# Two cache copies and a store of a decoder step, issued at another place of its program

## The chip, the cores and the metric

The kernel runs on one core of a Trainium2 chip. The metric is device time in microseconds of one execution. Five engines take part: TensorE (PE), VectorE (DVE), ScalarE (ACT), GpSimd (POOL) and SyncE (SP), which here issues most of the DMA transfers. Matrix products accumulate in eight PSUM banks, which the kernel shares out by tag.

## The reference

One step of a hybrid decoder layer. Every token gets a modulated RMS norm; `w_in` projects it; one branch is a matrix-memory recurrence (mLSTM), the other a sliding-window attention with sinks; both are gated, merged and projected. There are 1024 tokens of a prompt, and 8 samples of 4 tokens, each with a cache of 128 keys and values.

```python
def sink_attend(q, k, v, q_pos, k_pos, sinks):
    ...
    s = jnp.where(mask[None, :, None, None], s, -jnp.inf)
    mx = jnp.maximum(jnp.max(s, axis=-1, keepdims=True), sink)
    p = jnp.exp(s - mx)
    den = jnp.sum(p, axis=-1, keepdims=True) + jnp.exp(sink - mx)
    o = jnp.einsum('bnkgqs,bnskd->bnqkgd', p / den, v.astype(f32))

def layer(x, c, C0, n0, m0, k_past, v_past, ...):
    ...
    else:
        cw = k_past.shape[1]
        kk = jnp.concatenate([k_past.astype(k.dtype), k], axis=1)
        vv = jnp.concatenate([v_past.astype(v.dtype), v], axis=1)
        ...
        k_keep, v_keep = kk[:, -cw:], vv[:, -cw:]
```

What the change touches is the last line for the samples: the new caches `k_s` and `v_s` are the last 124 rows of the old ones, followed by the 4 new keys or values. Nothing in the step reads `k_s` or `v_s` afterwards; they are outputs.

## The kernel before

Activations stand with channels on the 128 partitions and tokens along the free axis, in pieces of 384, 384 and 288 tokens (the last piece holds the samples' 32). Products run in split precision: each float32 operand is cast to a high part by ScalarE (`wh_`, `t3h`) and a low part by VectorE (`wl_`, `t3l`), and three products `h_h*wh`, `h_l*wh`, `h_h*wl` are summed.

TensorE's program is written out by hand: each projection (a "job", such as `g_aq` for the attention's queries or `g_mq`, `g_mk`, `g_mv` for the memory's) issues its products one by one, and after each the object `side` may let a piece of other work in. That other work consists of Python generators in streams ("a" for the attention, "m" for gates and heads, "g", "x", "s"). A `yield lag, bank` hands back a lag in a modelled time and the PSUM tag that the next piece needs; `side.tick()` lets a piece go when its lag is over. All TensorE instructions are chained in the order in which they are written.

Up to the projections of keys and values, VectorE's and ScalarE's instructions are chained in the same way. Then `V.on = S.on = False`: from there to the output projection, a scheduler of the compiler orders the two engines by dependencies and its own costs. The same holds for SP's transfers, of which `issue()` says only that each comes after the last TensorE instruction written so far. A transfer or an instruction that is moved in the program can therefore move others.

Three pieces matter. `kv_turn()` turns the values to row form (`vnD`), writes the last 128 keys and values of the prompt (`k_p`, `v_p`), and takes the samples' new keys and values, `kns` and `vns`, out of PSUM. `unit(g, b0)` is the attention of two blocks of 128 queries for one group of heads: it loads `uqv` (queries and values) and `ukv` (keys) from DRAM, computes `sc`, masks it on VectorE (`p<-sc,cst,sink`, the maxima in `mx`, then `nmx`), takes exponentials on ScalarE (`p<-p,nmx`), transposes (`pt`) and multiplies with the values (`oT`). `sample_attention()` does the like for all samples at once (`scs`, `ps`, `pts`, `os`, `ost`), and copies the result to `osm`.

The tags of PSUM that matter are "g" (two banks, in turn for the projections' pieces) and "o" (two banks: `pt` of the second half, `oT`, and from the heads' stage on `sc` too). The mLSTM heads load `hq`, `hk`, `hv`, and the normalised tokens `hb`, by SP.

SP's transfers and those that ScalarE issues take eight completion semaphores in turn; a transfer waits until the one eight before it has landed.

Of the kernel before, what the change touches and what calls it, by code (L numbers as in the profile page):

```python
# [173 lines left out]
def body(tc, a):  # L174
    nc = tc.nc
    with ExitStack() as ctx:
# [11 lines left out]
        def pb(shape, name):  # L188
            return ps.tile(shape, F32, tag="b", bufs=2, name=name)

        def po(shape, name):
            return ps.tile(shape, F32, tag="o", bufs=2, name=name)

        def ht(shape, name, dt=F32):
            return sp.tile(shape, dt, tag="half", bufs=50, name=name)
# [51 lines left out]
        def stores(src=None):  # L247

            for e in list(due):
                if e[0] <= side.now or (src is not None and e[1].tensor is src):  # L250
                    due.remove(e)
                    issue(*e[1:])

        def dma(out, in_, late=False):
            stores(in_.tensor)
            issue(out, in_, late)
# [3 lines left out]
        def issue(out, in_, late=False, eng=None):  # L260
            ins = (eng or nc.sync).dma_start(out, in_)  # L261
            ins = getattr(ins, "ins", ins)
            if eng is None and paced:
                no_sync(ins, [last["PE"]])
            if late:
                no_sync(ins, free)
                free.clear()
            free.append(ins)

        side = Side(stores, {"m": (2, 35.0), "a": (5,8.0), "x": (2, 0.0), "s": (1, 0.0), "g": (1, 0.0)}, 1.5)  # L270
        def mm(out, lhsT, rhs, start, stop, share=1, more=False):
            n = int(np.prod(rhs.shape[1:]))
            side.now += max(n, 250) / 2400 if rhs.dtype == F32R else max(n * 4 // share, 128) / 2400
            side.products += 1
            in_order(nc.tensor.matmul(out, lhsT, rhs, start=start, stop=stop, skip_group_check=more))  # L275

        def tr(out, in_, idn):
            side.now += 0.11
            side.products += 1
            in_order(nc.tensor.transpose(out, in_, idn))  # L280
# [516 lines left out]
        def kv_turn():  # L797
            kl, kTs, vT, kns, vns = at.pop("kl"), at["kTs"], at.pop("vT"), ht([128, 128], "kns")[:NS], at["vns"]
            for p, n in enumerate((3, 3, 2)):
                tp = pb([128, 3, 128], f"vtp{p}")  # L800
                for j in range(n):
                    tr(tp[:, j], vT[p][:, j * 128:(j + 1) * 128], ident)
                vn = ht([128, 3, 128], f"avn{p}")
                S.copy(vn[:, :n], tp[:, :n])
                dma(vnD[:, 3 * p:3 * p + n], vn[:, :n])
                if p < 2:
                    yield 4.0, "b"
            dma(a["v_p"], vn[:, 1])
            tp = pb([128, 3, 128], "kvtp")
            tr(tp[:, 0], kl[:, 128:256], ident)  # L810
            tr(tp[:NS, 1], kTs, ident)
            tr(tp[:NS, 2], vT[2][:, 256:288], ident)
            kn = ht([128, 128], "kl")
            V.tensor_copy(kn, tp[:, 0])
            V.tensor_copy(kns, tp[:NS, 1])
            V.tensor_copy(vns, tp[:NS, 2])
            dma(a["k_p"], kn)
            dma(a["k_s"][0:124], a["cache_k"][4:128])
            dma(a["v_s"][0:124], a["cache_v"][4:128])
            dma(a["k_s"][124:128].rearrange("t b e -> b t e"), kns)  # L820
            dma(a["v_s"][124:128].rearrange("t b e -> b t e"), vns)

        heads_done, samples_done, units_done, products_done, plain_ends = [], [], [], [], []
        oD = [dp.tile([128, SEQ], F32, name=f"oD{g}") for g in range(4)]
# [90 lines left out]
        def sample_attention():  # L915
            qpad, vns, kTs = at["qpad"], at["vns"], at["kTs"]
            kc, vc = ([ht([128, 4, 128], f"{n}{u}") for u in range(2)] for n in ("kc", "vc"))
            smask = ht([128, 2, WIN + NS], "smask")
            sinkr = cp.tile([128, 1], F32, name="sinkr")
            for u in range(2):  # L920
                dma(kc[u], a["cache_k"][:, 4 * u:4 * u + 4])
                dma(vc[u], a["cache_v"][:, 4 * u:4 * u + 4])
            dma(smask, a["smask"])
            dma(sinkr, a["sink_rows"])
            yield 12.0, "b"
            for u in range(2):
                tq = pb([128, 4, 128], f"kctp{u}")
                for j in range(4):
                    tr(tq[:, j], kc[u][:, j], ident)
                S.copy(kc[u], tq)  # L930
                yield 3.0, "b" if u == 0 else "o"
            sc = po([128, 2, WIN + NS], "scs")
            for u in range(2):
                for w in range(4):
                    b = u * 4 + w
                    qb = qpad[:, b].rearrange("p k g t -> p (k g t)")
                    r = slice(32 * w, 32 * w + 32)
                    mm(sc[r, u, 0:WIN], qb, kc[u][:, w], start=True, stop=True)
                    mm(sc[r, u, WIN:], qb, kTs, start=True, stop=True)
            p = ht([128, 2, WIN + NS], "ps")  # L940
            mx = cp.tile([128, 2], F32, name="mxs")
            for u in range(2):
                V.tensor_tensor_reduce(p[:, u], sc[:, u], smask[:, u], 1.0, sinkr, ALU.add, ALU.max,
                                       accum_out=mx[:, u:u + 1])
            nmx = cp.tile([128, 4], F32, name="nmxs")
            V.tensor_scalar(nmx[:, 0:2], mx, -1.0, None, op0=ALU.mult)
            V.tensor_scalar(nmx[:, 2:4], nmx[:, 0:2], sinkr, None, op0=ALU.add)
            den = cp.tile([128, 2], F32, name="dens")
            for u in range(2):
                S.activation(p[:, u], p[:, u], AF.Exp, bias=nmx[:, u:u + 1], accum_out=den[:, u:u + 1])  # L950
            S.activation(nmx[:, 2:4], nmx[:, 2:4], AF.Exp)
            V.tensor_tensor(den, den, nmx[:, 2:4], op=ALU.add)
            V.reciprocal(den, den)
            for u in range(2):
                V.tensor_scalar(p[:, u], p[:, u], den[:, u:u + 1], None, op0=ALU.mult)
            yield 10.0, "b"
            pt = pb([128, 4, 128], "pts")
            for u in range(2):
                tr(pt[:, u], p[:, u, 0:WIN], ident)
                tr(pt[:NS, 2 + u], p[:, u, WIN:], ident)  # L960
            pT = kc[0]
            S.copy(pT[:, 0:2], pt[:, 0:2])
            V.tensor_copy(pT[:NS, 2:4], pt[:NS, 2:4])
            yield 7.0, "o"
            o = po([128, 2, 128], "os")
            for u in range(2):
                for w in range(4):
                    r = slice(32 * w, 32 * w + 32)
                    mm(o[r, u], pT[:, u, r], vc[u][:, w], start=True, stop=False, share=4)
                for w in range(4):  # L970
                    r = slice(32 * w, 32 * w + 32)
                    mm(o[r, u], pT[:NS, 2 + u, r], vns, start=False, stop=True, share=4)
            S.copy(p[:, :, 0:128], o)
            yield 4.0, "b"
            ot = pb([128, 2, 128], "ost")
            for u in range(2):
                tr(ot[:, u], p[:, u, 0:128], ident)
            for u in range(2):
                v4 = lambda t: t.rearrange("p (w k g t) -> p w k g t", k=2, g=4, t=NT)
                for kv, r in enumerate(half_rows):  # L980
                    V.tensor_copy(osm[r, :, 16 * u:16 * u + 16].rearrange("p g (w t) -> p w g t", t=NT), v4(ot[r, u])[:, :, kv])
            samples_done.append("a")
# [944 lines left out]
        for p, (c0, n) in enumerate(PARTS):  # L1927
            if p == 2:
                dma(hD[:, :, SEQ:T], xS)
            else:  # L1930
                for k in range(KT):
                    dma(hD[:, k, c0:c0 + n], xT[p][k])
        side.add("m", gates(gp, zg, gbias), "")
        side.add("a", kv_turn(), "b")
        V.on = S.on = False
        paced.append(True)
# [111 lines left out]
        for g in range(4):  # L2048
            queries(g)
        side.add("s", sample_attention(), "b")  # L2050
        for h in range(NH):
            head_jobs(h)
# [324 lines left out]
```

## Time and profile before

| | us |
|---|---|
| median of 3 runs | 823.74 |
| lowest and highest | 823.18, 823.78 |
| the profiled execution, time | 823.38 |
| its span in the trace | 821.6 |
| TensorE busy | 803.5 |
| VectorE, ScalarE, GpSimd busy | 598.6, 419.5, 45.8 |

The profiled execution lies 0.36 us below the median, and 1.78 us of it lie outside the span. All times inside the execution are counted from the span's start. A row of a timeline gives the start, the busy time, the engine (SPq is SP's queue of transfers, whose time is that of issuing, not of moving the data), the line, the operation and its tiles, a count where like instructions are merged, and in brackets how long the engine stood before it and for whom. Line 220 is the helper through which VectorE and ScalarE are called, 261 that of the transfers, 275 and 280 those of TensorE's products and transposes.

### The profile page before, as it was taken

The page shows a single profiled execution, that of the slowest core. Times are in us where ns is not written, and L with a number is a line of the kernel's source. Part 1 is how long each engine was busy: PE and PEld are TensorE (multiplying, and loading weights), DVE is VectorE, ACT ScalarE, POOL GpSimd, SP SyncE. Part 2 cuts the span into 40 slices and gives each one's busy share as a digit, 9 for nine tenths or more (in the row PEclk, how much of TensorE's full clock was granted, in tenths as well). Part 3 has the DMA queues.
Part 4 walks back from the last instruction along what each step waited for, and adds up shares of the span by engine and source line. Part 5 has one row for each costly group of instructions (what it writes and reads, how often), then busy time and mean ns, then how long its engine had stood idle before and what let it go on. Part 6 is the DMA issues. An engine that isn't in the chain of part 4 may idle for free.

```text
span 821.6 us, 15097 instructions
## 1 busy us (share of the span) xinstructions
PE 803.5 (98%) x5145; PEld 666.4 (81%) x5145; DVE 598.6 (73%) x1495; ACT 419.5 (51%) x1020; POOL 45.8 (6%) x111
## 2 busy tenths in 40 slices
PE   6999999999999999999999999999999999999996
PEld 3779898888788878888888878788888789997775
DVE  4799886756755557475657889898668997876666
ACT  5764355656565564546555545554446652224334
POOL 0120000000000000000001011010002101000000
PEclk9999999999999999999999999999999999999998
DMA  9995756546545415437765685864435789647632
GB/s 332 374 333 159 227 164 211 178 153 212 171 138 174 145 59 160 160 136 255 238 213 145 238 265 184 265 217 141 141 104 179 241 303 375 228 137 284 205 104 109
DMA packets 113473, 165.49 MB, mean 201 GB/s; under 512 B 21184, under 2 KB 55744, under 8 KB 113364
## 3 DMA queue, kind: packets, MB, share of 16 engines
q1 hardware_dynamic: 107748, 153.78, 56.9%
q10 hardware_dynamic: 4176, 6.56, 2.2%
q0 software_dynamic: 1472, 4.20, 1.4%
q8 instruction: 40, 0.66, 0.3%
q14 instruction: 37, 0.30, 0.1%
HBM read 115.51 MB, written 50.00 MB: 201 GB/s over the span
## 4 chain that ended last, share of the span: by engine, by line
PE 90%; DVE 5%; DMA 2%; issue 2%; ACT 1%; SPq 0%; DVEq 0%; ACTq 0%
PE by L275 12%; PE bx L275 11%; PE bw L275 11%; PE g_w_mo L275 6%; PE bz L275 5%; PE g_mq L275 3%; PE g_aq L275 3%; PE foW L275 3%; PE foX L275 2%; PE foY L275 2%; PE smp L275 2%; PE sc L275 2%; PE oT L275 2%; PE pt L280 2%; PE n L275 2%
## 5 line engine op out<-in xcount | busy, mean ns | idle before, releaser
L220 ACT ACTIVATE p<-p,nmx 128x256 f32<-128x256 f32 (+1 forms) x64 | 31.1, 486 | 17.7 <-DVE nmx L220 17.7
L220 DVE CUSTOM_DVE_ANT_0 p<-sc,cst,sink 128x256 f32<-128x256 f32 (+1 forms) x64 | 26.1, 462 | 9.2 <-PE sc L275 9.1
L275 PE MATMUL g_aq<-h_h,wh_aq 128*128 128x384 f32 (+1 forms) x96 | 32.2, 336 | 0.0
L275 PE MATMUL g_aq<-h_h,wl_aq 128*128 128x384 f32 (+1 forms) x96 | 30.9, 322 | 0.0
L275 PE MATMUL g_aq<-h_l,wh_aq 128*128 128x384 f32 (+1 forms) x96 | 30.9, 321 | 0.0
L275 PE MATMUL g_w_mo<-ym_h,wh_w_mo 128*128 128x384 f32 (+1 forms) x96 | 30.8, 321 | 0.0
L275 PE MATMUL g_w_mo<-ym_l,wh_w_mo 128*128 128x384 f32 (+1 forms) x96 | 30.8, 321 | 0.0
L275 PE MATMUL g_w_mo<-ym_l,wl_w_mo 128*128 128x384 f32 (+1 forms) x96 | 30.8, 321 | 0.0
L220 DVE COPY p<-pt 128x512 f32<-128x512 f32 (+1 forms) x16 | 10.5, 657 | 16.9 <-PE pt L280 16.8
L220 ACT CAST wosh<-wor 128x512 fp32r<-128x512 f32 x24 | 14.8, 621 | 12.6 <-DVE wor L220 12.6
L275 PEld LDWEIGHTS g_aq<-h_h,wh_aq 128*128 128x128 f32 x96 | 18.0, 188 | 2.5 <-issue 1.5
L261 POOL DMA_DIRECT2D oD<-uqv x16 | 8.8, 552 | 183.1 <-ACT uqv L220 169.9
L220 DVE SCALAR_TENSOR_TENSOR tgw_mo<-tgw_mo,g_w_mo 128x384 f32<-128x384 f32 (+1 forms) x24 | 12.4, 518 | 8.8 <-PE g_w_mo L275 7.9
L220 DVE TENSOR_TENSOR wosl<-wor,wosh 128x512 fp32r<-128x512 f32 x24 | 16.5, 686 | 2.8 <-ACT wosh L220 2.7
L275 PE MATMUL sc<-ukv,uqv 64*128 64x256 f32 (+1 forms) x128 | 18.0, 390 | 0.5 <-DMA ukv<-kD 0.5
L275 PEld LDWEIGHTS g_aq<-h_l,wh_aq 128*128 128x128 f32 x96 | 18.1, 188 | 0.0
L275 PEld LDWEIGHTS g_w_mo<-ym_l,wh_w_mo 128*128 128x128 f32 x96 | 18.0, 188 | 0.0
L275 PEld LDWEIGHTS g_w_mo<-ym_h,wh_w_mo 128*128 128x128 f32 x96 | 18.0, 188 | 0.0
L275 PEld LDWEIGHTS g_aq<-h_h,wl_aq 128*128 128x128 f32 x96 | 18.0, 188 | 0.0
L275 PEld LDWEIGHTS g_w_mo<-ym_l,wl_w_mo 128*128 128x128 f32 x96 | 18.0, 188 | 0.0
L220 DVE TENSOR_TENSOR et<-et,S 128x384 f32<-128x384 f32 (+1 forms) x12 | 6.1, 509 | 15.8 <-PE S L275 15.8
L275 PE MATMUL g_mq<-h_h,wh_mq 128*128 128x384 f32 (+1 forms) x48 | 16.8, 350 | 0.3 <-ACT mk L220 0.3
(2063 smaller groups left out, 2807.5 us busy)
## 6 DMA issues: line engine op xcount, KB each, us to landing
x<-xT SPq DMA_DIRECT2D x16, 256.0 KB
early_h<-w_ada SPq DMA_DIRECT2D x8, 512.0 KB
adar_ga<-w_ada SPq DMA_DIRECT2D x16, 256.0 KB
wr_ga<-w SPq DMA_DIRECT2D x16, 256.0 KB
wr_gm<-w SPq DMA_DIRECT2D x16, 256.0 KB
taD<-gt SPq DMA_DIRECT2D x16, 256.0 KB
tmD<-gt SPq DMA_DIRECT2D x16, 256.0 KB
wor<-w_out SPq DMA_DIRECT2D x16, 256.0 KB
```

The costliest lines, as they stand in the source:

```text
L220: ins = f(*args, **kw)
L261: ins = (eng or nc.sync).dma_start(out, in_)
L275: in_order(nc.tensor.matmul(out, lhsT, rhs, start=start, stop=stop, skip_group_check=more))
L280: in_order(nc.tensor.transpose(out, in_, idn))
```

## The change

Three of the transfers at the end of `kv_turn()` are now issued in `sample_attention()`, after the probabilities are normalised and before they are transposed. The store of `kns` stays.

```diff
@@ kv_turn()
             V.tensor_copy(kns, tp[:NS, 1])
             V.tensor_copy(vns, tp[:NS, 2])
             dma(a["k_p"], kn)
-            dma(a["k_s"][0:124], a["cache_k"][4:128])
-            dma(a["v_s"][0:124], a["cache_v"][4:128])
             dma(a["k_s"][124:128].rearrange("t b e -> b t e"), kns)
-            dma(a["v_s"][124:128].rearrange("t b e -> b t e"), vns)
@@ sample_attention()
             for u in range(2):
                 V.tensor_scalar(p[:, u], p[:, u], den[:, u:u + 1], None, op0=ALU.mult)
             yield 10.0, "b"
+            dma(a["k_s"][0:124], a["cache_k"][4:128])
+            dma(a["v_s"][0:124], a["cache_v"][4:128])
+            dma(a["v_s"][124:128].rearrange("t b e -> b t e"), vns)
             pt = pb([128, 4, 128], "pts")
             for u in range(2):
                 tr(pt[:, u], p[:, u, 0:WIN], ident)
```

The number of instructions is the same, and TensorE's and GpSimd's orders are the same. SP, VectorE and ScalarE have other orders.

On SP at the old place (`wr_aq` are weights of the fourth query group, `qD` the queries' home in DRAM, `adar_ga` weights of the modulation), before:

```order
L261 DMA k_s<-cache_k 16x7936
L261 DMA vnD<-avn_967 128x256
L261 DMA v_p<-avn_967 128x128
L261 DMA k_p<-kl 128x128
L261 DMA v_s<-cache_v 16x7936
L261 DMA k_s<-kns 8x4x128
L261 DMA v_s<-vns 8x4x128
L261 DMA adar_ga_984<-w_ada 128x512
L261 DMA wr_aq_0_1018<-w 128x512
L261 DMA wr_aq_1_1020<-w 128x512
L261 DMA qD_114<-aqr 128x384 x2
L261 DMA qD_114<-aqr 128x256
```

And now:

```order
L261 DMA wr_aq_0_1015<-w 128x512
L261 DMA wr_aq_1_1017<-w 128x512
L261 DMA vnD<-avn_967 128x256
L261 DMA v_p<-avn_967 128x128
L261 DMA k_p<-kl 128x128
L261 DMA k_s<-kns 8x4x128
L261 DMA adar_ga_981<-w_ada 128x512
L261 DMA qD_114<-aqr 128x384 x2
L261 DMA uqv<-vnD 128x256
L261 DMA qD_114<-aqr 128x256
```

The three transfers are gone, the two loads of `wr_aq` stand in the place of the first copy, and the stores of `qD` come that much sooner. On SP at the new place the copies of `k_s` and `v_s` and the store of `vns` stand directly ahead of the loads of `wr_mk`, behind the `uqv` and `ukv` loads of the unit before; the rows after that are the same.

On ScalarE at the unit (0, 4) (`t3h` is the high part of a combination of tokens that the later heads' product needs), before:

```order
L220 ACTIVATE p_1306<-p_1306,den 128x256 x2
L220 COPY p_1199<-pt_0_0_1448 128x384
L220 ACTIVATE aq<-g_aq_1413 128x384
L220 CAST t3h_1368<-x_6_96 128x512
L220 COPY uqv<-oT_0_1520 128x256
L220 ACTIVATE p_1482,den<-p_1482,nmx 128x256
```

And now:

```order
L220 COPY p_1196<-pt_0_0_1445 128x384
L220 ACTIVATE p_1303<-p_1303,den 128x256 x2
L220 ACTIVATE aq<-g_aq_1410 128x384
L220 COPY uqv<-oT_0_1517 128x256
L220 CAST t3h_1365<-x_6_96 128x512
L220 ACTIVATE p_1479,den<-p_1479,nmx 128x256
```

The cast of `t3h` and the copy that takes `oT` out of PSUM have changed places. VectorE's order there is the same: `t3l`, which needs `t3h`, and behind it the two `nmx`.

On VectorE at the unit (2, 4) (`p_2516` and `p_2517` are the two halves of its `p`; ISA is the masking), before, from its third masking on:

```order
L220 ISA p_2517,mx<-sc_4_1_2520,cst,sink 128x256
L220 ISA mx 128x1
L220 TENSOR_TENSOR hb_0_2450<-hb_0_2450,hb_0_2448 128x512
L220 ISA p_2517,mx<-sc_4_1_2520,cst,sink 128x256
L220 ISA mx 128x1
L220 TENSOR_TENSOR wr_mv_0_2417<-wr_mk_0_2413,wr_mv_0_2417 128x512
L220 TENSOR_TENSOR hb_1_2454<-hb_1_2454,hb_1_2452 128x512
L220 TENSOR_SCALAR nmx<-mx 128x4
L220 TENSOR_TENSOR nmx<-sink,mx 128x4
L220 TENSOR_TENSOR wr_mk_0_2413<-ws_2561,wr_mk_0_2413 128x512
L220 COPY osm<-ost 64x4x4x4 x4
```

And now:

```order
L220 TENSOR_TENSOR wr_mv_0_2417<-wr_mk_0_2413,wr_mv_0_2417 128x512
L220 TENSOR_TENSOR wr_mk_0_2413<-ws_2561,wr_mk_0_2413 128x512
L220 COPY osm<-ost 64x4x4x4 x2
L220 TENSOR_TENSOR wl_phead_in_6__2566<-wr_mk_0_2413,wh_phead_in_6__2565 128x512
L220 COPY osm<-ost 64x4x4x4 x2
L220 ISA p_2516,mx<-sc_4_0_2519,cst,sink 128x256
L220 ISA mx 128x1
L220 ISA p_2516,mx<-sc_4_0_2519,cst,sink 128x256
L220 ISA mx 128x1
L220 TENSOR_TENSOR hb_0_2450<-hb_0_2450,hb_0_2448 128x512
L220 ISA p_2517,mx<-sc_4_1_2520,cst,sink 128x256
```

The maskings of this unit have gone behind the copies of `osm`, and the subtractions `wr_mv`, `wr_mk` and `wl` in front of them.

## The prediction

> **What bounds the kernel now.** I read the page first, for the engines and the chain that ended last, then the stretches, then TensorE's waits, and then the timelines around the old and the new place of the moved lines.
>
> ```profile
> span 821.6 us, 15097 instructions
> PE 803.5 (98%) x5145; PEld 666.4 (81%) x5145; DVE 598.6 (73%) x1495; ACT 419.5 (51%) x1020; POOL 45.8 (6%) x111
> PE 90%; DVE 5%; DMA 2%; issue 2%; ACT 1%; SPq 0%; DVEq 0%; ACTq 0%
> ```
>
> TensorE is busy 803.5 us of 821.6; the chain is TensorE's for nine tenths. A change that leaves TensorE's instructions and their order alone can only alter the 18.1 us in which it stands. Where it stands, the busy time by stretch shows (columns: stretch, its length, then busy time and count of PE, PEld, DVE, ACT, POOL, the granted clock, DMA's share, GB/s):
>
> ```profile
> 0.00:20.00 20.00, 12.75 (x77) 6.13 (x77) 9.41 (x36) 10.30 (x17) 0.53 (x5) 1.00 0.92 330
> 93.00:165.00 72.00, 71.66 (x509) 60.49 (x507) 56.05 (x204) 40.64 (x126) 3.06 (x6) 1.00 0.61 195
> 180.00:205.00 25.00, 24.98 (x235) 20.90 (x232) 14.46 (x47) 14.01 (x44) 1.94 (x5) 1.00 0.70 223
> ```
>
> The start takes 7.2 us of them, far from the change. Between 93 and 165 us TensorE stands 0.34 us, between 180 and 205 us not at all. So there is hardly anything to gain there, and whatever makes TensorE wait there is lost in full. One wait lies beside the old place, in the list of TensorE's waits (us in total, times, longest) and in the chain in order of time (start, us):
>
> ```profile
> PE sc L275 <- DMA ukv<-kD: 0.5, 1, 0.5
> 84.06 5.35 DMA qD<-aqr
> 89.85 2.31 DMA ukv<-kD
> ```
>
> The first unit of the prompt's attention waits for its keys, which were asked for behind its queries, which were read back after their own store.
>
> **The removal, and the wait that goes.** SP's own timeline at the old place, and TensorE's last product before the wait:
>
> ```profile
> 72.37 0.81 SPq L261 DMA_DIRECT2D k_s<-cache_k  x1
> 78.14 0.32 SPq L261 DMA_DIRECT2D vnD<-avn  x1
> 80.33 0.55 SPq L261 DMA_DIRECT2D v_s<-cache_v  x1
> 80.97 0.82 SPq L261 DMA_DIRECT2D k_s<-kns  x1
> 81.89 0.70 SPq L261 DMA_DIRECT2D v_s<-vns  x1
> 83.13 0.89 SPq L261 DMA_DIRECT2D wr_aq<-w  x2
> 84.06 1.45 SPq L261 DMA_DIRECT2D qD<-aqr  x3
> 91.45 0.34 PE L275 MATMUL g_aq<-h_h,wl_aq 128*128 128x384 f32 x1
> 92.29 0.93 PE L275 MATMUL sc<-ukv,uqv 64*128 64x128 f32 x8 [0.50 <-DMA ukv<-kD]
> ```
>
> Between 80.33 and 84.06 SP loses v_s's copy (0.64 us to the next start) and the store of vns (0.80); the two wr_aq loads (0.93) move up into the place of the first copy at 72.4, where SP then had nothing to issue until 78.14. So the stores of qD go out about 0.64 + 0.80 + 0.93 = 2.4 us earlier, near 81.7. Taking the same 5.35 us to land, the first lands at 87.0, the reads follow at 87.1 and 87.4, and the keys land 2.31 us later, at 89.7. That is 2 us ahead of 91.79, where the last product of g_aq ends. Were the third store of qD (the last of the 1.45 us, at 85.1) held to its present time by VectorE's rotation, the reads behind it could still go out from 85.6. The whole wait goes: **-0.5 us**, all that the row shows. The other end is nothing, if the keys were as late as now, for which no row speaks.
>
> **What the compiler's own order does with it: ScalarE at 118 us.** ScalarE's and VectorE's orders are chosen by a scheduler here, and moving three transfers moved them too. TensorE's order is the same row for row. The rows of before, at the unit (0, 4):
>
> ```profile
> 112.53 0.61 ACT L220 CAST t3h<-x 128x512 fp32r<-128x512 f32 x1
> 117.91 0.37 ACT L220 COPY uqv<-oT 128x256 f32<-128x256 f32 x1 [4.78 <-PE oT L275]
> 118.18 0.51 ACT L220 ACTIVATE p<-p,nmx 128x256 f32<-128x256 f32 x1
> 121.98 0.48 ACT L220 ACTIVATE aq<-g_aq 128x384 f32<-128x384 f32 x1
> 117.11 0.69 DVE L220 TENSOR_TENSOR t3l<-x,t3h 128x512 fp32r<-128x512 f32 x1
> 117.72 0.16 DVE L220 TENSOR_SCALAR nmx<-mx 128x4 f32<-128x4 f32 x1
> 122.94 0.34 PE L275 MATMUL g_mq<-h_h,wh_mq 128*128 128x384 f32 x1
> ```
>
> Before, ScalarE casts t3h and then stands 4.78 us for TensorE's oT. Now the cast is queued behind the copy that waits for oT. It starts at 117.91 + 0.27 = 118.18 and ends at 118.79. VectorE's t3l, which subtracts it, starts there and not at 117.11: 1.7 us later. nmx is queued behind t3l, 117.72 becomes 119.4, and the exponentials, which need nmx, start at about 119.6 in place of 118.18, 1.44 us later. From there ScalarE's work is one unbroken run to the evacuation aq<-g_aq at 121.98, which therefore comes at 123.4 and ends 0.48 us later, 123.9. It frees one of the two "g" banks, and the first product of g_mq at 122.94 is written into that bank. Before, 122.94 - 122.46 = 0.48 us were spare; now TensorE stands 1.44 - 0.48 = **+1.0 us**. The upper end is 1.7 - 0.48 = 1.2, if the run does not make good what VectorE's lag adds; the lower is 0, if a part of ScalarE's run has room that records laid end to end do not show. I take 1.0, since each row of the run follows the one ahead without a wait. The half microsecond won at 92 us does not shrink it: oT comes from TensorE, and all of this moves with it.
>
> **The same at the new place: VectorE at 197 us.** Rows of before, VectorE's and then TensorE's:
>
> ```profile
> 192.44 0.48 DVE L220 CUSTOM_DVE_ANT_0 p<-sc,cst,sink 128x256 f32<-128x256 f32 x1 [0.81 <-PE sc L275]
> 195.00 0.69 DVE L220 TENSOR_TENSOR hb<-hb,hb 128x512 f32<-128x512 f32 x1 [1.26 <-DMA hb<-hD]
> 195.61 0.48 DVE L220 CUSTOM_DVE_ANT_0 p<-sc,cst,sink 128x256 f32<-128x256 f32 x1
> 197.96 0.92 DVE L220 COPY osm<-ost 64x64 f32<-64x64 f32 x4
> 199.39 0.68 DVE L220 TENSOR_TENSOR wl_phead_in__2566<-wr_mk,wh_phead_in__2565 128x512 fp32r<-128x512 f32 x1
> 196.15 0.38 PE L280 MATMUL ost<-cst,ps 128*128 128x128 f32 x2
> 198.58 0.88 PE L275 MATMUL oT<-p,uqv 128*64 128x128 f32 x12
> 199.38 1.09 PE L280 MATMUL pt<-cst,p 128*128 128x128 f32 x8
> ```
>
> Before, the four maskings of sc for the unit (2, 4) came first (192.44 to 196.0) and the four copies of osm after them. Now the four copies and the subtraction wl stand ahead of the maskings. The copies need TensorE's ost, which is there at 196.15 + 0.38 = 196.5. Then two copies (0.23 each), wl (0.60, its pitch), two copies: 196.57 + 0.46 + 0.60 + 0.46 = 198.1, and the first two maskings (0.41 each) end at 198.9. They free the "o" bank that oT takes at 198.58, so it starts at about 199.05: +0.47. Behind them hb (0.61) and the last two maskings: 200.35, which free the bank of pt's second half. Its fifth transpose was due at 199.8, with the shift 200.3, so another 0.1. Together **+0.6 us**; between 0.3 (ost and the copies a little earlier) and 1.0 (each wait for another engine in the row adding 0.1).
>
> **The moved transfers themselves.** They cost no compute time; what they push back is SP's queue. SP runs ahead of TensorE, so they go out not beside the transposes of p at 181 us, but at about 171. Its timeline there, one row of the list of SP's waits, and TensorE's first use of hk:
>
> ```profile
> 170.99 2.36 SPq L261 DMA_DIRECT2D wr_mk<-w  x2
> 179.69 0.80 SPq L261 DMA_DIRECT2D wr_mv<-w  x2
> 181.06 0.38 SPq L261 DMA_DIRECT2D hq<-qD  x1
> 187.58 0.32 SPq L261 DMA_DIRECT2D et<-nmd  x1
> 188.52 2.10 SPq L261 DMA_DIRECT2D hb<-hD  x4
> SPq L261 <- DMA vD<-mk: 11.9, 3, 6.3
> 202.82 0.49 PE L280 MATMUL tk<-cst,hk 128*128 128x128 f32 x3
> ```
>
> Each transfer waits for an older one to land: SP stood 11.9 us in three waits for ScalarE's stores vD<-mk, the longest from 173.4 to 179.69, another ahead of 187.58. Three more transfers in front shift which one meets which wait. The copies take the places of the wr_mk loads, the store of vns that of wr_mv; wr_mk goes out near 180.5, wr_mv near 181.4, and hq, hk, hv meet the wait that et met, so hq goes out at 187.6 instead of 181.06. All but hb have room: wr_mk and wr_mv land by 187.5 even at the 6.0 us of hb, ahead of VectorE's maskings at 192.44, and hk is first used at 202.82. hb's second load now goes out at 189.0 (the second of four in 2.10 us) and VectorE gets it at 195.00; with hq, hk, hv put in front of it (3 x 0.47) it goes out at 190.4, and with the same 6.0 us lands at 196.4. VectorE reaches it at 198.9, as worked out above. **0 us**, with 2.5 us to spare; if that cover is gone, each us beyond it is one for TensorE.
>
> By the Trainium skill ("DMA: Bandwidth & Descriptors", Anatomy of one DMA) a transfer takes about 2.0 us plus its bytes over 436 GB/s, fitted there for GpSimd's path; for the 0.25 MB of hb that would be 2.6 us, and the cover 5.9 us. The trace does not agree at this place: 6.0 us beside other loads, so I hold to the row.
>
> Sum: -0.5 + 1.0 + 0.6 + 0 = **+1.1 us**. The profiled execution took 823.38 us (span 821.6 and 1.78 around it), which would become 824.5; it lies 0.36 below the median of 823.74, so the median becomes **824.8 us**.
>
> **Rivals.**
> *hb comes late (slower).* The three loads put behind 187.5 are 0.56 MB; at the 223 GB/s of that stretch they take 2.5 us, all of the room. If hb's loads queue behind them, they land at 196.4 + 2.5 = 198.9, just where VectorE arrives, and the stores and units of that time push them beyond. The half-landed hb stands ahead of the last two maskings, so each us goes straight to TensorE's pt. One to three us more, 2 taken: 826.8. For it: before, VectorE already stood 1.26 us for this load. Against it: VectorE comes 3.9 us later than before.
>
> *The order costs nothing, the gain stays.* If t3h's lag is absorbed in ScalarE's run and the maskings in VectorE's, only the wait at 92 us goes: 823.2. Against it, TensorE's missing idle time in both stretches.
>
> *The change doesn't do what it says.* The copies land beside nothing that waits, before and after, and the schedule's differences cancel: 823.7.
>
> I see no row by which it could be faster by more than the 0.57 us of the one wait near the change; only a schedule that unfolds differently further on could.
>
> **How the numbers follow.** A measurement of this kernel can tell about 0.2% (1.65 us) from no change: between 822.1 and 825.4 is "same". My forecast has 0.55: its own range, from -0.5 + 0 + 0.3 to -0.4 + 1.2 + 1.0, is 823.5 to 825.5, and with unmodelled waits a third of it lies above 825.4. hb late has 0.25, only the gain 0.12, no effect 0.08. Slower by over 0.2% is then 0.18 + 0.25 = 0.43; faster 0.05 for a schedule that I have not followed; the rest, 0.52, is the same. The range for 8 in 10 runs from the gain alone, 823.2, to hb late by two, 826.8.
>
> **What would show it.** Right: no TensorE wait for ukv near 92 us; a wait of g_mq for ScalarE's aq of about 1 us near 123; sc's maskings of the unit (2, 4) behind osm, and waits of oT and pt for VectorE of together 0.6 near 199; hq at 187 or later. Wrong: no wait at 123 (then t3h's swap was harmless), a wait of VectorE for hb at 199 (the rival), a wait for ukv that stays, or new TensorE waits beyond 215 us.

## The result, and the profile after

The changed kernel takes 824.86 us (median of 21 runs, 824.04 to 826.09), the kernel before on the same chips 823.41 us (21 runs, 822.76 to 824.07): 1.45 us more, a ratio of 1.0017 with a 95% interval of 1.0011 to 1.0023, or 0.9 to 1.9 us. The profiled execution took 825.05 us.

The page of the changed kernel, its engines and its chain:

```profile
span 823.3 us, 15101 instructions
PE 804.1 (98%) x5145; PEld 666.2 (81%) x5145; DVE 599.5 (73%) x1495; ACT 419.2 (51%) x1020; POOL 45.7 (6%) x111
PE 93%; DVE 3%; issue 1%; DMA 1%; ACT 1%; SPq 0%; DVEq 0%; ACTq 0%
```

Each engine's count of instructions is the same as before, and its busy time within 0.9 us; the total differs by 4 that are in none of the five counts. DMA has lost half of its 2% of the chain. TensorE's waits (us in total, times, longest) show what came for it; the row for ukv is gone, and two are new:

```profile
PE g_mq L275 <- ACT aq L220: 0.9, 1, 0.9
PE oT L275 <- DVE mx L220: 0.5, 1, 0.5
```

At the old place, SP's timeline and the first product of the prompt's attention:

```profile
72.80 1.14 SPq L261 DMA_DIRECT2D wr_aq<-w  x2
82.14 0.90 SPq L261 DMA_DIRECT2D qD<-aqr  x2
85.39 0.32 SPq L261 DMA_DIRECT2D uqv<-qD  x1
85.76 0.42 SPq L261 DMA_DIRECT2D ukv<-kD  x1
92.14 0.93 PE L275 MATMUL sc<-ukv,uqv 64*128 64x128 f32 x8
```

In this execution the first loads came later, and TensorE ran 0.43 us behind the execution of before when it reached the product ahead of sc, so each time here is to be read with that. The keys are asked for at 85.76 instead of 89.85, and by the trace's semaphore events (a transfer's landing raises one) they have landed at 88.14, 4.0 us ahead of sc. sc starts at 92.14 with no wait: seen with the 0.43, 0.57 us earlier than at 92.29. Then ScalarE, VectorE and TensorE around 118 to 124 us:

```profile
117.75 0.37 ACT L220 COPY uqv<-oT 128x256 f32<-128x256 f32 x1 [3.53 <-PE oT L275]
118.01 0.62 ACT L220 CAST t3h<-x 128x512 fp32r<-128x512 f32 x1
119.47 0.51 ACT L220 ACTIVATE p<-p,nmx 128x256 f32<-128x256 f32 x1 [0.84 <-DVE nmx L220]
123.27 0.47 ACT L220 ACTIVATE aq<-g_aq 128x384 f32<-128x384 f32 x1
118.67 0.69 DVE L220 TENSOR_TENSOR t3l<-x,t3h 128x512 fp32r<-128x512 f32 x1 [0.55 <-ACT t3h L220]
119.28 0.16 DVE L220 TENSOR_SCALAR nmx<-mx 128x4 f32<-128x4 f32 x1
123.80 0.44 PE L275 MATMUL g_mq<-h_h,wh_mq 128*128 128x384 f32 x1 [0.86 <-ACT aq L220]
```

Each link that the prediction named can be read here: the cast behind oT's copy, t3l waiting for it, nmx behind t3l, the exponentials waiting for nmx, and the evacuation of aq at 123.27, for which TensorE stands. g_mq starts 0.86 us later than before, though TensorE had been 0.15 earlier up to there: 1.01 us lost. The next product follows g_mq's first one after 0.28 us instead of 0.18, so 0.10 more is lost right behind the wait, and from there TensorE runs 0.96 us late. And at 197 to 201 us:

```profile
197.53 0.46 DVE L220 COPY osm<-ost 64x64 f32<-64x64 f32 x2 [0.55 <-PE ost L280]
198.00 0.69 DVE L220 TENSOR_TENSOR wl_phead_in__2566<-wr_mk,wh_phead_in__2565 128x512 fp32r<-128x512 f32 x1
198.71 0.46 DVE L220 COPY osm<-ost 64x64 f32<-64x64 f32 x2
199.18 0.48 DVE L220 CUSTOM_DVE_ANT_0 p<-sc,cst,sink 128x256 f32<-128x256 f32 x1
199.99 0.69 DVE L220 TENSOR_TENSOR hb<-hb,hb 128x512 f32<-128x512 f32 x1
201.69 0.69 DVE L220 TENSOR_TENSOR hb<-hb,hb 128x512 f32<-128x512 f32 x1 [0.20 <-DMA hb<-hD]
200.13 0.88 PE L275 MATMUL oT<-p,uqv 128*64 128x128 f32 x12 [0.52 <-DVE mx L220]
200.94 1.26 PE L280 MATMUL pt<-cst,p 128*128 128x128 f32 x8
```

oT starts 1.55 us later than before, 0.59 more than the 0.96; and pt, whose eight transposes take 1.26 instead of 1.09, adds 0.17. VectorE also stands 0.20 us for hb at 201.69, which TensorE doesn't feel. From there to the end TensorE's lag is 1.7 us, the difference of the two spans (823.3 - 821.6). So of the 1.7 us of these two executions, 0.43 is the start, -0.57 the wait that went, +1.11 and +0.76 the two new places. Without the start, which is not the change's, the three places add up to +1.3 us, against 1.45 by the medians.

### The profile page after: what moved, and what is told of

It reads as the page before. It is cut to its first block, busy times and chain, and to the rows that moved or that the text cites. A ratio compares the mean times of both kernels' runs of the same rounds, so it can differ in the third digit from the quotient of the medians.

```text
span 823.3 us, 15101 instructions
## 1 busy us (share of the span) xinstructions
PE 804.1 (98%) x5145; PEld 666.2 (81%) x5145; DVE 599.5 (73%) x1495; ACT 419.2 (51%) x1020; POOL 45.7 (6%) x111
## 4 chain that ended last, share of the span: by engine, by line
PE 93%; DVE 3%; issue 1%; DMA 1%; ACT 1%; SPq 0%; DVEq 0%; ACTq 0%
PE by L275 12%; PE bx L275 11%; PE bw L275 11%; PE g_aq L275 6%; PE g_w_mo L275 6%; PE bz L275 5%; PE g_mq L275 3%; PE foW L275 3%; PE foX L275 2%; PE foY L275 2%; PE smp L275 2%; PE sc L275 2%; PE oT L275 2%; PE pt L280 2%; PE n L275 2%; PE g_ak L275 2%
```

## The experiments

Each kernel was timed in five rounds beside the kernel before; "before" below is its median in the same rounds (823.54 for the first four, 823.36 for the next four, 823.42 for the last three). Where an order is put back, this is done with a dependency that says "this instruction after that one" on the same engine and moves no data. Half a microsecond lies near the width of the intervals, so where a loss sits is read from the traces, by how far TensorE runs behind the execution of before on either side of a place.

### One order put back: the cast

```diff
 def block_split(n, k, t):
     S.copy(hi, t)
+    pin[n, k] = S.before
 ...
     S.copy(o, oT...)
+    if (g, b0) == (0, 0): no_sync(S.before, [pin["t3", 2]])
```

> The changed kernel, with one order put back: ScalarE's cast of t3h ahead of its copy uqv<-oT at 118 us; all else as changed. Theory (the scheduler's orders cost, the transfers do not): TensorE's wait of 0.9 to 1.0 us for aq near 123 us goes, the two near 200 us stay; 1.0 us less than the changed kernel, 0.4 to 0.5 above the kernel before. Rival (the wait at 123 us comes from the earlier transfers, the swap is only beside it): time as the changed kernel, 1.4 us above before. Second rival (the time moves on: another evacuation is late next): less than 0.5 us gained.

Measured: 824.13 us against 823.54, a ratio of 1.0007 (0.9998 to 1.0015), so +0.59 in place of +1.45; the interval includes no change. TensorE's waits:

```profile
PE oT L276 <- DVE mx L221: 0.5, 1, 0.5
PE g_mq L276 <- ACT aq L221: 0.2, 1, 0.2
```

The wait at 123 us falls from 0.9 to 0.2, that of oT stays. By TensorE's start of g_mq, 0.37 of the 1.01 us is still lost there (with the product behind it, 0.48 of 1.11). The theory holds in its main part; the remainder is a cause that it did not have.

### The other order put back: osm behind the maskings

```diff
 def unit(g, b0):
     ...
+    pin["sc", g, b0] = V.before
 def sample_attention():
     ...
         V.tensor_copy(osm[...], ...)
+        no_sync(V.before, [pin["sc", 2, 4]])
```

> The changed kernel, with the copies of osm put back behind VectorE's last masking of the unit (2, 4). Theory: the waits of oT and pt for mx near 200 us (0.52 and 0.2 or so in the changed kernel, 0.86 by TensorE's shift) go, that near 123 us stays; 0.8 us less than the changed kernel, about 0.5 to 0.6 above before. VectorE then reaches hb near 198.8, ahead of its landing at 199.4, and waits about 0.6 us for it; the last masking is done by 200.5, before pt's second half needs it, so TensorE should not feel it. Rival (hb's late loads are what costs here): the same 0.8 us are lost again, now to hb, and the time is that of the changed kernel.

Measured: 824.13 against 823.54, +0.59 by the medians; the ratio on record is 1.0011 (1.0002 to 1.002), or 0.2 to 1.6 us. In its trace TensorE no longer waits at all around 200 us, and VectorE waits only 0.2 us for hb, not 0.6:

```profile
DVE hb L221 <- DMA hb<-hD: 0.2, 1, 0.2
```

Of the 0.76 us, 0.1 is left, in pt's transposes (1.22 us instead of 1.09). So the loss at 200 us was the order, as expected; hb did not take it back.

### Both put back

The two edits together.

> The changed kernel with both orders put back. Theory: only the gain at 92 us is left, 0.5 us below the kernel before (ratio 0.9994), 1.9 below the changed one. Rival (late transfers cost by themselves): not below the kernel before.

Measured: 823.44 against 823.54, 0.9999 (0.999 to 1.0007): the loss is gone, but the gain of 0.5 doesn't show in full. The trace says why. ScalarE, VectorE and TensorE near 112 to 123 us, and VectorE's wait for hb:

```profile
112.33 0.91 ACT L221 ACTIVATE p<-p,den 128x256 f32<-128x256 f32 x2 [1.87 <-DVE den L221]
113.14 0.47 ACT L221 ACTIVATE aq<-g_aq 128x384 f32<-128x384 f32 x1
113.65 0.59 DVE L221 STREAM_SHUFFLE ropet<-aq 128x384 f32<-128x384 f32 x1
122.56 0.44 PE L276 MATMUL g_mq<-h_h,wh_mq 128*128 128x384 f32 x1 [0.23 <-ACT aq L221]
DVE hb L221 <- DMA hb<-hD: 0.7, 1, 0.7
```

An earlier evacuation of aq, at 113.14, comes late behind p<-p,den, which waited 1.87 us for VectorE's den; VectorE's rotation then waits for that aq, its maskings and t3l follow late, and the same chain to g_mq runs 0.37 us late even with the cast in its old place, and 0.1 more is lost in the product behind the wait. Behind hb's 0.7 us TensorE loses 0.1. Together these take back the 0.57 won at 92 us. Behind den stands an order of VectorE's that had also changed, from 106 us on, and ahead of all of it one pair on ScalarE: the cast of wh_mq now came before an evacuation of aq. The pair in the kernel before, and in the changed one:

```profile
103.74 0.49 ACT L220 ACTIVATE aq<-g_aq 128x384 f32<-128x384 f32 x1 [1.20 <-PE g_aq L275]
105.58 0.62 ACT L220 CAST wh_mq<-wr_mq 128x512 fp32r<-128x512 f32 x1 [1.35 <-PE g_aq L275]
```

```profile
105.42 0.62 ACT L220 CAST wh_mq<-wr_mq 128x512 fp32r<-128x512 f32 x1 [3.05 <-PE g_aq L275]
105.94 0.48 ACT L220 ACTIVATE aq<-g_aq 128x384 f32<-128x384 f32 x1
```

The evacuation now stands behind a cast that waits 3.05 us, and comes 2.2 us later.

### Only the store of vns moved

```diff
-            dma(a["v_s"][124:128]..., vns)        # kv_turn
+            dma(a["v_s"][124:128]..., vns)        # sample_attention; both copies stay
```

> The kernel before with only the store of vns moved to the samples' attention; both copies stay at the old place. ScalarE's and VectorE's orders at 118 and 197 us are those of before. SP's qD stores go out 0.8 us earlier, the copies' data are still ahead of them. Theory: the keys land 0.8 us earlier, at 91.35, which is ahead of 91.79; the whole wait of 0.5 us goes, time 0.4 to 0.5 below before. Rival (data ahead in the rings, not SP's issue time, sets the landing of qD): qD lands as late as before, the wait stays at 0.3 to 0.5, time as before.

Measured: 823.13 against 823.54, 0.9996 (0.9987 to 1.0005). Its trace has no wait for ukv; SP's reads and TensorE's sc (this execution runs 0.45 us late from its start):

```profile
89.29 0.32 SPq L261 DMA_DIRECT2D uqv<-qD  x1
89.66 0.42 SPq L261 DMA_DIRECT2D ukv<-kD  x1
92.17 0.93 PE L275 MATMUL sc<-ukv,uqv 64*128 64x128 f32 x8
```

TensorE gains 0.57 us there, and both orders are those of before. One of the three moved transfers is thus enough for the whole gain in this execution. It is a narrow one: by the semaphore events the keys landed at 91.80, 0.4 us ahead of sc, where the changed kernel has 4.0 us. The 0.4 us of the medians lies inside what the timing can tell, so only the trace shows the gain.

### One pair put back

```diff
 def split4(raw, name, ...):
     S.copy(hi, raw)
+    if name == "mq0_0": no_sync(S.before, [pin["aq", 2, 1]])
```

`pin["aq", 2, 1]` is the evacuation that the cast had overtaken.

> The changed kernel with one single order given: ScalarE's cast of wh_mq (first half) behind the evacuation of the last but one piece before it, as in the kernel before. With that one pair put back, ScalarE's and VectorE's orders up to 130 us are again those of before in every row; the order at 197 us stays as changed. Theory (the loss at 123 us is one disturbed pair and what the scheduler makes of it; the cast t3h alone was 0.6 to 0.7 of it, and the late aq ahead of it 0.3 to 0.4): TensorE's wait for aq at 123 us goes entirely, 1.0 us less than the changed kernel, 0.3 to 0.4 above before. Rival (the 0.2 us wait that stayed with t3h put back has another cause, such as the transfers): 0.2 to 0.4 of it stay.

Measured: 823.57 against 823.36, 1.0002 (0.9993 to 1.0011), +0.21. In the list of TensorE's waits there is no aq any more, only the old wait of 0.3 for mk and the new one of oT:

```profile
PE oT L276 <- DVE mx L221: 0.5, 1, 0.5
PE g_mq L276 <- ACT mk L221: 0.3, 1, 0.3
```

TensorE loses nothing at 123 us, and ScalarE's and VectorE's orders up to 187 us are those of before in every row. So all of the 1.11 us there hangs on that one pair; the scheduler made the rest of it, the cast of t3h included. At 200 us the 0.76 are lost as in the changed kernel.

### That pair and osm put back

The edit holds a third order too, that of the cast of t3h, as in the first experiment. The run with the pair alone has this order without being told, so it adds nothing at 118 us.

> That order and the one of osm behind the maskings, both given. Theory: the gain of 0.54 us at 92 us, no wait at 123, at most 0.2 us at 200 us, where VectorE waits for hb ahead of its last masking: 0.3 to 0.5 us below the kernel before. Rival: not below before, because something else of the late transfers costs 0.4.

Measured: 823.09 against 823.36, 0.9998 (0.9989 to 1.0007). In the trace TensorE gains 0.57 us at 92 us, loses nothing at 123 and 0.13 at 200; the medians' -0.27 cannot be told from no change. With the transfers at their new place and these orders put back, next to nothing is lost.

### No transfers at all

The three lines are left out; k_s and v_s do not get the caches' old rows nor v_s the new values.

> The kernel before without the three transfers at all (the caches' copies and the samples' new values are left out of the outputs k_s and v_s). ScalarE's and VectorE's orders at 118 us are those of the changed kernel, at 197 us those of before. Theory (transfers cost nothing, orders do): the wait at 92 us goes, that at 123 us is there in full, none at 200 us: -0.54 + 1.0 = 0.4 to 0.5 us above the kernel before, although it does less. Rival (the transfers themselves cost): below the kernel before.

Measured: 824.33 against 823.36, 1.0011 (1.0003 to 1.002). A kernel with 1 MB less to copy is slower than before, because its ScalarE order is that of the changed kernel:

```profile
PE g_mq L275 <- ACT aq L220: 0.9, 1, 0.9
```

Its trace gives -0.57 at 92 us, +1.11 at 123, and nothing at 200; the median's +0.97 is above the 0.5 expected, by less than its interval's half-width.

### The copies issued by GpSimd

```diff
-            dma(a["k_s"][0:124], a["cache_k"][4:128])
+            issue(a["k_s"][0:124], a["cache_k"][4:128], eng=nc.gpsimd)      # v_s alike
```

> The kernel before with the two copies issued by GpSimd at their old place in the program, the store of vns by SP as before. ScalarE's and VectorE's orders are those of the kernel without the transfers, in nearly every row. Theory: SP is rid of the copies' place, so the keys come early enough though the copies' data still move at 72 to 85 us: time as the kernel without the transfers, 0.4 to 0.5 above before. Rival (the copies' data beside the stores of qD keep them late): a wait for ukv at 92 us of up to 0.5 stays, 0.9 to 1.0 above before.

Measured: 827.42 against 823.36, 1.005 (1.0037 to 1.0063): a miss. The experiment was not what it was meant to be. On GpSimd the copies wait for nothing, so they went out at the very start, beside the first loads; GpSimd's row, ScalarE's first row that needs a load, and TensorE's first wait:

```profile
1.32 0.64 POOL L261 DMA_DIRECT2D k_s<-cache_k  x1 [0.27 <-issue]
9.90 0.42 ACT L220 ACTIVATE xsq<-small 128x256 f32<-128x256 f32 x1 [7.87 <-DMA small<-small]
PE xc L275 <- ACT xsq L220: 10.4, 1, 10.4
```

ScalarE gets its first input at 9.90, before at 6.11. After that the trace has the same steps as the others: no wait for ukv at 92 us, 1.1 us lost at 123. It says nothing on whether the copies' data delay qD.

### How much cover is left at hb

The order of every engine is that of the changed kernel; one or two extra copies of 0.5 MB into a spare buffer move ahead of hb's loads.

```diff
 issue(oD[g][:, c0:c0 + 256], o, eng=nc.gpsimd)
+if (g, b0) == (1, 6):        # one or both
+    issue(spare_k, a["cache_k"][4:128], eng=nc.gpsimd)
+    issue(spare_v, a["cache_v"][4:128], eng=nc.gpsimd)
```

> The changed kernel with one more transfer of 0.5 MB (cache_k into a spare buffer in DRAM), issued by GpSimd behind its store oD at 187.6 us, so that it moves just ahead of and beside hb's loads; every engine's order is that of the changed kernel. It asks how much cover the change left at hb. Theory (in the changed kernel hb's second load lands 0.54 us before VectorE takes it, and behind it two maskings go straight to TensorE's pt): the copy alone moved about 3.5 us at 72 to 76 us; sharing the engines, it delays hb by 2 us, VectorE waits 1.5, TensorE's pt as much: 1 to 2 us above the changed kernel, 2.5 to 3.5 above before. Rival (hb has room, the rival of the prediction never was near): time as the changed kernel.

> The same with two transfers, 1 MB in all. Theory: hb 4 us later, VectorE's wait 3.5 us, nearly all of it TensorE's: 3 to 4 us above the changed kernel. Rival: as the changed kernel, or no more than with the half.

Measured: with one copy 826.76, with two 825.73, against 823.42; ratios 1.0043 (1.0029 to 1.0056) and 1.0028 (1.0016 to 1.004), so 1.9 and 0.9 us above the changed kernel. VectorE's hb and TensorE's pt in the traces with one copy, then with two:

```profile
201.28 0.69 DVE L220 TENSOR_TENSOR hb<-hb,hb 128x512 f32<-128x512 f32 x1 [0.61 <-DMA hb<-hD]
202.83 0.66 PE L280 MATMUL pt<-cst,p 128*128 128x128 f32 x4 [0.65 <-DVE mx L220]
```

```profile
199.51 0.69 DVE L220 TENSOR_TENSOR hb<-hb,hb 128x512 f32<-128x512 f32 x1 [0.19 <-DMA hb<-hD]
201.07 0.66 PE L280 MATMUL pt<-cst,p 128*128 128x128 f32 x4 [0.22 <-DVE mx L220]
```

The mechanism is as stated: what VectorE waits for hb, TensorE waits at pt, nearly one for one, and no cover is left beyond some tenths. The sizes were wrong: 0.5 MB delays hb by about 1 us, not 2, and the double dose by less, because in that execution the store vD<-mk landed earlier and SP's loads went out sooner. With five and six runs the two intervals overlap, so the doses are not told apart. The traces show 0.7 and 0.2 us of the 1.9 and 0.9, and each is a single execution: that with one copy also loses 0.9 us near 54 us, long before the copy, to a load of wg, and that with two is the fastest of its six. Where the rest of the medians goes is open.

> The kernel before with the same two transfers of 0.5 MB at the same place; its orders are those of before. There VectorE takes hb at 195.0 and the last masking behind it ends at 196.0, while TensorE's pt needs its bank at 199.8: 3.8 us of cover. Theory: hb 3 to 4 us later, so VectorE waits 4 to 5 us instead of 1.3, and TensorE loses 0 to 0.5 us. The difference from the same dose in the changed kernel (3 to 4) is cover that the change used up. Rival (transfers beside TensorE's work slow it down by themselves, whatever the order): as much lost as in the changed kernel.

Measured: 824.94 against 823.42, 1.0018 (1.0009 to 1.0027), +1.5. VectorE's hb, ScalarE's exponentials and TensorE's wait:

```profile
198.61 0.69 DVE L220 TENSOR_TENSOR hb<-hb,hb 128x512 f32<-128x512 f32 x1 [4.75 <-DMA hb<-hD]
201.80 0.51 ACT L220 ACTIVATE p<-p,nmx 128x256 f32<-128x256 f32 x1 [6.77 <-DVE nmx L220]
205.28 0.55 PE L280 MATMUL tv<-cst,hv 128*128 128x128 f32 x3 [1.39 <-ACT p L220]
```

VectorE waits 4.75 us for hb, as expected, and pt is not held up. But nmx is queued behind hb, the exponentials behind nmx, ScalarE's copy of pt behind them, and tv needs the bank that this copy frees. The cover counted to pt, 3.8 us, was not the shortest. So the expected contrast between the kernels, 0.5 against 3 to 4, is not there; the medians are +1.5 and +0.9 for the same dose. That is the number the rival expected, though the trace shows a queue behind hb and no general slowing of TensorE. That the change used up cover at hb is not shown by the times; it is read from the waits at pt alone. The orders up to the copies are those of before, and TensorE waits 0.97 us for ukv at 92 us here instead of 0.50: that wait differs between executions.

## Why the prediction was right, and where it was off

**The wait at 92 us**: -0.5 was forecast, -0.57 measured, and the stores of qD went out at the forecast time (82.14, or 81.7 without the late start). The spare time was under-read: 2 us were forecast, and the keys had 4.0. The forecast of 5.35 us for the qD stores was long: with less in front of them the read followed 3.25 us after the first store. With only the store of vns moved, and so both copies and the loads of wr_aq still in front, it followed after 5.60 us.

**ScalarE at 118 us**: +1.0 forecast, 1.01 measured at the wait and 1.11 with the product behind it, with every link of the chain in the trace. One step of the reading was too narrow. The cast of t3h was named as the cause; with it put back, 0.37 us stayed, and one earlier pair (wh_mq ahead of aq) carries the whole. The prediction traced the path that ended last and took the rest of the order as harmless.

**VectorE at 197 us**: +0.6 forecast, 0.76 measured (0.59 at oT, 0.17 at pt). The term was a little undersized: between the copies the subtraction wl takes 0.71 us (198.00 to 198.71) where 0.60, its pitch among its like, was used. That is 0.11 of the 0.12 us by which the maskings begin late, at 199.18; the forecast, 198.1 moved by TensorE's lag of 0.96, was 199.06.

**The moved transfers**: 0 forecast, and 0 measured: with the orders put back the changed place costs nothing that can be told. But the cover of 2.5 us for hb was mis-sized. SP's rows of the changed kernel:

```profile
189.66 0.33 SPq L261 DMA_DIRECT2D hq<-qD  x1
191.98 3.02 SPq L261 DMA_DIRECT2D hb<-hD  x4
```

SP could send hq only at 189.66 (forecast, moved by 0.96: 188.6), because the store vD<-mk that it waits for took 4.2 us to land instead of 3.1. hb's second load, sent at 192.47, took 7.0 us where 6.0 was taken from the row before; the trace's semaphore events have it landed at 199.45, 0.54 us before VectorE took it. The estimate of 2.6 us that the prediction worked out from the fit of the Trainium skill ("DMA: Bandwidth & Descriptors", Anatomy of one DMA), which the page gives for GpSimd's path, was further off than the row. The rival that made it late by two lost by that half microsecond, not by the 3.9 us that were counted against it.

**The rivals**: "the order costs nothing" falls by the runs with the orders put back; "no effect" by the sum. The sum, +1.1, was below the 1.45 measured and inside its interval; the traces' three places give +1.3. The time, 824.8, is 0.06 us off, and that is luck: the change was forecast 0.35 us too small, and the 823.74 of three runs that it was added to lies 0.33 us above the 823.41 of the 21.

## What to carry to other kernels

Where a scheduler orders the engines, compare the orders before counting transfers: here 1 MB of copies cost nothing at its new place, and at the old one half a microsecond only together with a store of 16 KB, while one swapped pair on an engine that is busy half the time cost twice what the move gained. Follow a moved instruction to every bank it frees, and count the cover of the shortest of these ways, not of the first. And look whether a smaller edit gives the same gain: moving that store alone removed the wait, though with 0.4 us to spare instead of 4.0.

## What was not expected of the hardware

The copies that GpSimd issued at 1.32 us delayed a load that SP issued at 1.65 by 3.8 us (ScalarE took it at 9.90 instead of 6.11): here a queue of its own did not set a transfer apart. The Trainium skill ("DMA: Bandwidth & Descriptors", Issuing engines are not separate DMA queues) says that transfers of all issuing engines run on the same 16 DMA engines; this trace agrees in that the load came 3.8 us late, and does not show which of them moved what. The second load of hb, 0.25 MB, landed 5.9 us after its issue in the kernel before, 7.0 in the changed one, and 6.6 and 8.6 us with one and two extra copies beside it; with two copies in the kernel before it took 9.55. The bytes alone do not set it. What else does is only in part in these traces: two copies beside it come with the longest times, but one copy with a shorter time than none.
